# The MLP's first layer by one level of Strassen's method, with adding transfers, in four chunks

## The chip, the cores and the metric

One core of a Trainium2 chip runs the whole block for 512 tokens. The metric is the device time of one execution in microseconds (us): a median of 813.45 over 3 runs (813.43 to 813.47). Engines: TensorE (PE, with its weight loads PEld), VectorE (DVE), ScalarE (ACT), GpSimd (POOL), SyncE (SP, which only issues transfers).

## The reference

```python
h  = rmsnorm(x, norm_mix_g)
u, v, bg, cg, xs, ga, gb = split(h @ w_in)              # w_in: 1024 x 7168
a  = gelu(u) * (masked w_s @ rmsnorm(gelu(v)) + b_s)    # per 128-token block
c  = bg * causal_dwconv3(cg * xs)
m  = sigmoid(ga) * (a @ w_proj_a) + sigmoid(gb) * (c @ w_proj_b)
x  = x + m @ w_out
hf = rmsnorm(x, norm_ff_g)
z  = relu(hf @ w_ff1)                                   # w_ff1: 1024 x 4096
x  = x + (z * z) @ w_ff2                                # w_ff2: 4096 x 1024
return rmsnorm(x, norm_final_g)
```

All arrays are float32. x is 512 x 1024.

## The kernel before

Channels lie on the 128 partitions and the 512 tokens along the free axis, so a layer is a row of output tiles of 128 channels x 512 tokens, each summed over k tiles of 128 input channels. A float32 operand is carried as two float32r parts, hi (rounded) and lo (the rest), and a product is three matmuls: hi x hi, hi x lo of the activations, lo x hi (lines 120 to 122).

A weight *unit* is a 1024 x 128 block, one [128, 1024] tile: eight k tiles for one output tile, 24 matmuls. `prep` (line 97) loads it on SyncE's queue, ScalarE casts it to `whi` (line 84) and VectorE subtracts for `wlo` (line 85). `unit_matmuls` preps the unit it needs and two more ahead. Every engine takes its instructions in the order in which they stand on it.

The program goes through v, u with spatial gating, branch A's gate and projection, branch B, its gate and projection, the output projection (8 units), and the MLP. The MLP runs in `NCH` = 2 chunks of 16 hidden tiles. In a chunk the first layer makes 16 tiles: one unit each, then VectorE's ReLU times the token scale `Rf` out of PSUM (`t_z`, line 367), ScalarE's square (line 369) and the split into `zh` and `zl`. Then the second layer makes 8 output tiles from two units each and adds them to `res` (line 475). `x2h` and `x2l` (line 357) are the split input of the first layer. `Rf` comes from the sum of squares through `rstd_of` and `spread`, with a power on GpSimd (line 134). The last output tile is made in two halves of 256 tokens (`last_tile`, lines 424 to 426), so that the final norm of one half runs beside the other.

PSUM has seven banks in rotation and one for statistics. SBUF tiles are shared by phases through tags.

Of the kernel before, what the change touches and what calls it, by code (L numbers as in the profile page):

```python
# [8 lines left out]
F32 = mybir.dt.float32  # L9
# [12 lines left out]
NCH = 2  # L22
CF = FT // NCH
EPS = 1e-6
N_WARM = 10

# Columns of the packed per-channel vectors.
# [4 lines left out]
def hybrid_block(ctx, tc, xT, vecs, w_v, w_main, w_s, b_s, out_a, out_b):  # L32
# [12 lines left out]
    outp = ctx.enter_context(tc.tile_pool(name="outp", bufs=4))  # L45
# [4 lines left out]
    # ---------------------------------------------------------------- constants  # L50
# [14 lines left out]
    # TensorE reaches its full clock while the first loads are under way.  # L65
# [27 lines left out]
    # Every unit is [128 (k in tile), 8 (k tile), 128 (m)].  # L93
    n_units = w_main.shape[0]
    parts = {}

    def prep(i):
        if i >= n_units or i in parts:
            return
        r = raws.tile([P, KT * P], F32, name="raw")  # L100
        nc.sync.dma_start(r, w_main[i])
        hi = wsp.tile([P, KT * P], F32R, name="whi")
        lo = wsp.tile([P, KT * P], F32R, name="wlo")
        split_into(hi, lo, r)
        parts[i] = (hi, lo)

    state = {"next": 0}
    AHEAD = 2

    def unit_matmuls(psum, act_hi, act_lo, start=True, stop=True, cols=slice(0, S)):  # L110
        """psum += W_unit.T @ act over the unit's 8 k tiles."""
        i = state["next"]
        state["next"] += 1
        prep(i)
        for a in range(1, AHEAD + 1):
            prep(i + a)
        hi, lo = parts.pop(i)
        for k in range(KT):
            ks = slice(k * P, (k + 1) * P)
            nc.tensor.matmul(psum, hi[:, ks], act_hi[k][:, cols], start=start and k == 0, stop=False)  # L120
            nc.tensor.matmul(psum, hi[:, ks], act_lo[k][:, cols], start=False, stop=False)  # L121
            nc.tensor.matmul(psum, lo[:, ks], act_hi[k][:, cols], start=False, stop=stop and k == KT - 1)  # L122
# [14 lines left out]
    def rstd_of(acc, lo=0, n=NB):  # L137
        """Mean over partitions of acc's columns, as [token, block]; then rstd."""
# [7 lines left out]
    def spread(r, n=NB):  # L146
        """rstd as [token, block] -> [any partition, token], in PSUM."""
# [10 lines left out]
    xh = [shared("X", 16, f"xh{k}", F32R) for k in range(KT)]  # L158
    xl = [shared("X", 16, f"xl{k}", F32R) for k in range(KT)]
    acc = shared("acc", 1, "acc")  # L160
    vt = [[shared("V", 8, f"vt{b}{h}") for h in range(2)] for b in range(NB)]
    wsT = [shared("M", 16, f"wsT{i}").rearrange("p (g i) -> p g i", i=P) for i in range(2)]
    bsb = [shared("M", 16, f"bsb{i}").rearrange("p (g i) -> p g i", i=P) for i in range(2)]
    vsum = small.tile([P, 2, NB], F32, name="vsum")

    vparts = {}

    def prep_v(i):
        if i >= 2 * KT:
            prep(i - 2 * KT)  # L170
            return
# [3 lines left out]
        t = raws.tile([P, KT * P], F32, name="raw")[:, :HALF]  # L175
        nc.sync.dma_start(t, w_v[h, k])
        vh = shared("M", 16, f"vh{h}{k}", F32R)
        vl = shared("M", 16, f"vl{h}{k}", F32R)
# [30 lines left out]
    for i in range(2 * KT):  # L209
# [57 lines left out]
    def mix(g):  # L267
        pm = bank()
        for b in range(NB):
            nc.tensor.matmul(  # L270
                pm[:, b * P : (b + 1) * P], vt[b][g // 4][:, (g % 4) * P : (g % 4 + 1) * P], wsT[g // 4][:, g % 4, :],
# [5 lines left out]
            bsb[g // 4][:, g % 4 : g % 4 + 1, :].broadcast_to([P, NB, P]), op0=ALU.mult, op1=ALU.add,  # L277
# [43 lines left out]
    # ---------------------------------------------------------------- branch A's gate and projection  # L321
    m1 = [shared("V", 8, f"m1{k}") for k in range(KT)]
# [15 lines left out]
    mh = [shared("M", 16, f"mh{k}", F32R) for k in range(KT)]  # L338
    ml = [shared("M", 16, f"ml{k}", F32R) for k in range(KT)]
# [9 lines left out]
    # ---------------------------------------------------------------- output projection, residual  # L349
    xh2 = [shared("X", 16, f"x2h{k}", F32R) for k in range(KT)]  # L350
    xl2 = [shared("X", 16, f"x2l{k}", F32R) for k in range(KT)]
    acc = shared("acc", 1, "accb")
    for j in range(KT):
# [186 lines left out]
```

## Time and profile before

| | before |
|---|---|
| median of 3 runs | 813.45 us |
| span of the profiled execution | 811.9 us |
| granted TensorE clock, mean | 0.997 |
| first layer of the first chunk (456.0 to 545.4) | 89.4 us, TensorE busy throughout |
| second layer of the first chunk (545.4 to 632.4) | 87.0 us, TensorE busy throughout |
| mean DMA rate | 100 GB/s |

The span goes from the first to the last instruction; what lies around it (1.55 us against the median) has no rows. Busy times of PE are modelled from pipelined matmuls, so how far apart matmuls start says more than the duration of one.

### The profile page before, as it was taken

The page shows a single profiled execution, that of the slowest core. Times are in us where ns is not written, and L with a number is a line of the kernel's source. Part 1 is how long each engine was busy: PE and PEld are TensorE (multiplying, and loading weights), DVE is VectorE, ACT ScalarE, POOL GpSimd, SP SyncE. Part 2 cuts the span into 40 slices and gives each one's busy share as a digit, 9 for nine tenths or more (in the row PEclk, how much of TensorE's full clock was granted, in tenths as well). Part 3 has the DMA queues.
Part 4 walks back from the last instruction along what each step waited for, and adds up shares of the span by engine and source line. Part 5 has one row for each costly group of instructions (what it writes and reads, how often), then busy time and mean ns, then how long its engine had stood idle before and what let it go on. Part 6 is the DMA issues. An engine that isn't in the chain of part 4 may idle for free.

```text
span 811.9 us, 8874 instructions
## 1 busy us (share of the span) xinstructions
PE 804.2 (99%) x3646; PEld 667.2 (82%) x3646; DVE 376.0 (46%) x501; ACT 250.6 (31%) x324; POOL 6.1 (1%) x15
## 2 busy tenths in 40 slices
PE   9999999999999999999999999999999999999996
PEld 6888888888888888888888888888888888888886
DVE  7555653334555555444455554442233445434433
ACT  7323332222212222332344253332112334422221
POOL 0000000000000000000000000000000000000000
PEclk9999999999999999999999999999999999999998
DMA  7522223322332233233223223223322332233203
GB/s 247 195 105 104 78 77 105 104 90 92 104 104 82 100 105 103 79 104 103 93 89 105 97 84 105 101 81 104 103 93 89 105 103 85 97 104 104 79 0 105
DMA packets 25352, 81.35 MB, mean 100 GB/s; under 512 B 2768, under 2 KB 3792, under 8 KB 25312
## 3 DMA queue, kind: packets, MB, share of 16 engines
q1 hardware_dynamic: 24416, 79.18, 29.1%
q10 hardware_dynamic: 864, 1.57, 0.6%
q8 instruction: 28, 0.46, 0.3%
q14 instruction: 12, 0.10, 0.0%
q0 software_dynamic: 32, 0.03, 0.0%
HBM read 78.68 MB, written 2.10 MB: 99 GB/s over the span
## 4 chain that ended last, share of the span: by engine, by line
PE 98%; DMA 0%; ACT 0%; DVEq 0%; POOLq 0%; POOL 0%; DVE 0%; issue 0%
PE bank L121 30%; PE bank L120 30%; PE bank L122 30%; PE bank L219 5%; PE bank L270 1%; PE bank L425 0%; PE bank L426 0%; PE bank L424 0%; DMA res<-xT 0%; PE bank L152 0%; PE st L141 0%; DVEq L534 0%; PE bank L393 0%; PE st L441 0%; POOLq L534 0%; ACT xh L87 0%
## 5 line engine op out<-in xcount | busy, mean ns | idle before, releaser
L84 ACT CAST whi<-raw 128x1024 fp32r<-128x1024 f32 x136 | 143.4, 1054 | 494.2 <-PE bank L121 373.9
L85 DVE TENSOR_TENSOR wlo<-raw,whi 128x1024 fp32r<-128x1024 f32 x136 | 166.5, 1225 | 78.7 <-ACT whi L84 77.6
L120 PE MATMUL bank<-xh,whi 128*128 128x512 f32 x384 | 150.0, 391 | 0.0
L121 PE MATMUL bank<-xl,whi 128*128 128x512 f32 x384 | 149.4, 389 | 0.0
L122 PE MATMUL bank<-xh,wlo 128*128 128x512 f32 x384 | 149.4, 389 | 0.0
L120 PE MATMUL bank<-x2h,whi 128*128 128x512 f32 x256 | 99.8, 390 | 0.0
L122 PE MATMUL bank<-x2h,wlo 128*128 128x512 f32 x256 | 99.6, 389 | 0.0
L121 PE MATMUL bank<-x2l,whi 128*128 128x512 f32 x256 | 99.6, 389 | 0.0
L120 PE MATMUL bank<-zh,whi 128*128 128x512 f32 x240 | 93.4, 389 | 0.0
L121 PE MATMUL bank<-zl,whi 128*128 128x512 f32 x240 | 93.4, 389 | 0.0
L122 PE MATMUL bank<-zh,wlo 128*128 128x512 f32 x240 | 93.4, 389 | 0.0
L122 PEld LDWEIGHTS bank<-xh,wlo 128*128 128x128 f32 x384 | 72.1, 188 | 15.0
L120 PEld LDWEIGHTS bank<-xh,whi 128*128 128x128 f32 x384 | 72.2, 188 | 14.8
L121 PEld LDWEIGHTS bank<-xl,whi 128*128 128x128 f32 x384 | 72.1, 188 | 14.6
L367 DVE SCALAR_TENSOR_TENSOR t_z<-bank,Rf 128x512 f32<-128x512 f32 x32 | 22.0, 691 | 78.8 <-PE bank L122 78.8
L121 PEld LDWEIGHTS bank<-x2l,whi 128*128 128x128 f32 x256 | 48.1, 188 | 10.0
L122 PEld LDWEIGHTS bank<-x2h,wlo 128*128 128x128 f32 x256 | 48.1, 188 | 10.0
L120 PEld LDWEIGHTS bank<-x2h,whi 128*128 128x128 f32 x256 | 48.1, 188 | 9.9
L121 PEld LDWEIGHTS bank<-zl,whi 128*128 128x128 f32 x240 | 45.1, 188 | 9.4
L122 PEld LDWEIGHTS bank<-zh,wlo 128*128 128x128 f32 x240 | 45.1, 188 | 9.3
L120 PEld LDWEIGHTS bank<-zh,whi 128*128 128x128 f32 x240 | 45.1, 188 | 9.3
L475 DVE TENSOR_TENSOR res<-bank,res 128x512 f32<-128x512 f32 x15 | 10.4, 692 | 50.1 <-PE bank L122 50.1
(118 smaller groups left out, 818.6 us busy)
## 6 DMA issues: line engine op xcount, KB each, us to landing
raw<-w_main SPq DMA_DIRECT2D x136, 512.0 KB, 3.2
raw<-w_v SPq DMA_DIRECT2D x16, 256.0 KB, 4.0
res<-xT SPq DMA_DIRECT2D x8, 256.5 KB, 4.8
out_a<-o SPq DMA_DIRECT2D x4, 256.0 KB, 2.4
wsT<-w_sT ACTq DMA_DIRECT2D x2, 256.0 KB, 5.0
bsb<-b_sb ACTq DMA_DIRECT2D x2, 256.0 KB, 5.5
out_b<-ob ACTq DMA_DIRECT2D x2, 256.0 KB, 3.0
out_b<-ob SPq DMA_DIRECT2D x2, 256.0 KB, 3.1
```

The lines of the kernel that those rows point to most:

```text
L84: nc.scalar.copy(hi, src)
L85: nc.vector.tensor_tensor(lo, src, hi.bitcast(F32), op=ALU.subtract)
L120: nc.tensor.matmul(psum, hi[:, ks], act_hi[k][:, cols], start=start and k == 0, stop=False)
L121: nc.tensor.matmul(psum, hi[:, ks], act_lo[k][:, cols], start=False, stop=False)
L122: nc.tensor.matmul(psum, lo[:, ks], act_hi[k][:, cols], start=False, stop=stop and k == KT - 1)
L219: nc.tensor.matmul(vbanks[h][b], xs[k][:, b * P : (b + 1) * P], ws, start=k == 0 and ws is vh and xs is xh, stop=k == KT - 1 and xs is xl,)
L270: nc.tensor.matmul(pm[:, b * P : (b + 1) * P], vt[b][g // 4][:, (g % 4) * P : (g % 4 + 1) * P], wsT[g // 4][:, g % 4, :], start=True, stop ...
L367: nc.vector.scalar_tensor_tensor(t, pz, 0.0, Rf, op0=ALU.max, op1=ALU.mult)
L475: nc.vector.tensor_add(res[j], py, res[j])
```

## The change

The first layer's product W1^T x is cut into 2 x 2 blocks and made with 7 block products in place of 8, in the form with shared sums. Two output tiles of 128 channels, from a 1024 x 256 block of W1, are a *pair*; its four blocks are 512 x 128 (four slices of 128 input channels each, stored as `w_ff1[i]` = A12, A11, A22, A21, where the first index is the output tile and the second the half of the input channels). The right sides are the halves of the input channels x halves of the tokens, so every matmul has 256 columns.

- `combos` makes the right sides once, in the output projection, whose units come in the order 0, 4, 1, 5, ... so that both halves are at hand: B11, B21 and B22 as they are, and four sums (nT1, T3, nT2, nT4). Each is split in hi and lo.
- A pair has four *operands* of weights: raw A12 and A11; raw A22; and two tiles of sums. The two sums in `sm[0]` (a `wsum` tile) are made by transfers on GpSimd's queue: `build` copies A11 and A22 into it and then adds A21 to both with an adding transfer. The other two, in `sm[1]`, are made by VectorE (`add2`, lines 470 and 471). `wsum0` and `wsum2` take turns as targets of the transfers, `wsum1` and `wsum3` as VectorE's.
- `add_operand`, `pump` and `need` make the splits a list of steps, of which each product or unit takes one. At most `RING` = 4 operands are held.
- `block_pair` runs the seven products (`product`, 4 slices x 3 matmuls). The last one, P7, and what follows it, run after the next pair's P2 (`late`). Results leave PSUM through copies on ScalarE and sums on VectorE into `c1` and `c2`, and `z_evac` goes on from there in SBUF.
- The MLP has four chunks of 8 hidden tiles (4 pairs) and 8 second-layer units. Each chunk but the last also makes the first pair of the next. The last two output tiles, not one, are made in halves.
- A load on SyncE's queue now brings two units (1 MB), or three blocks of a pair (768 KB). `raws` has two such buffers.

```diff
-NCH = 2
+NCH = 4
+RING = 4
...
-    raws = ctx.enter_context(tc.tile_pool(name="raws", bufs=4))
-    wsp = ctx.enter_context(tc.tile_pool(name="wsp", bufs=3))
+    raws = ctx.enter_context(tc.tile_pool(name="raws", bufs=2))
+    wsp = ctx.enter_context(tc.tile_pool(name="wsp", bufs=RING))
...
+    def add_operand(src, n=2, last=None):
+        o = {"done": False, "ready": False, "idx": len(opnds)}
+        def step():
+            hi = wsp.tile([P, n, S], F32R, name="whi", padded_shape=[P, 2, S])
+            lo = wsp.tile([P, n, S], F32R, name="wlo", padded_shape=[P, 2, S])
+            split_into(hi, lo, src())
+            o["hi"], o["lo"], o["ready"] = hi, lo, True
+            if last:
+                load_after(last)
+        opnds.append(o)
+        steps.append((step, o))
+        return o
+
+    def pump(n=1):
+        while steps and n:
+            step, o = steps[0]
+            if o is not None and o["idx"] >= RING and not opnds[o["idx"] - RING]["done"]:
+                return
+            steps.pop(0)
+            step()
+            n -= 1
...
+    def build(i):
+        if i < NP1:
+            t = sums_t[2 * (i % 2)]
+            nc.gpsimd.dma_start(t, w_ff1[i, :, 1:3, :])
+            nc.gpsimd.dma_start(t, w_ff1[i, :, 3:4, :].broadcast_to([P, 2, S]), accum_op=ALU.add)
...
+            def add2(raw=raw, sm=sm, key=key):
+                nc.vector.tensor_tensor(sm[1][:, 1, :], sm[0][:, 1, :], raw(1, 2)[:, 0, :], op=ALU.add)
+                nc.vector.tensor_tensor(sm[1][:, 0, :], sm[1][:, 1, :], raw(0, 1)[:, 0, :], op=ALU.add)
+                load_after(key)
+            tl = []
+            tl.append(add_operand(lambda raw=raw: raw(0, 2)))
+            tl.append(add_operand(lambda raw=raw: raw(2, 3), n=1))
+            steps.append((add2, None))
+            tl.append(add_operand(lambda sm=sm: sm[1]))
+            tl.append(add_operand(lambda sm=sm: sm[0]))
+            steps.append((lambda i=i: build(i + 2), None))
+            pairs.append(tl)
+
+    LEFT = {"P1": (0, 1, "B11"), "P2": (0, 0, "B21"), "D": (1, 0, "nT4"), "F": (2, 0, "B22"),
+            "P6": (2, 1, "nT2"), "E": (3, 1, "nT1"), "P7": (3, 0, "T3")}
+
+    def product(p, name, out, first, last=False):
+        t, g, r = LEFT[name]
+        o = pairs[p][t]
+        pump()
+        need(o)
+        for sl in range(KS):
+            c = slice(sl * P, (sl + 1) * P)
+            w_hi, w_lo = o["hi"][:, g, c], o["lo"][:, g, c]
+            x_hi, x_lo = right[r, sl, 0], right[r, sl, 1]
+            nc.tensor.matmul(out, w_hi, x_hi, start=first and sl == 0, stop=False, skip_group_check=True)
+            nc.tensor.matmul(out, w_hi, x_lo, start=False, stop=False, skip_group_check=True)
+            nc.tensor.matmul(out, w_lo, x_hi, start=False, stop=sl == KS - 1, skip_group_check=True)
+        if name in ("P2", "D", "P6", "P7"):
+            o["done"] = True
...
+    def block_pair(p, after):
+        ba, bf, bd = bank(), bank(), bank()
+        A, P2 = ba[:, :N2], ba[:, N2:]
+        F = bf[:, :N2]
+        Dp, E = bd[:, :N2], bd[:, N2:]
+        c1, c2 = temp("c1"), temp("c2")
+        product(p, "P1", A, True)
+        product(p, "P2", P2, False)
+        nc.scalar.copy(c1[:, :N2], A)
+        nc.vector.tensor_add(c1[:, :N2], P2, c1[:, :N2])
+        flush_late()
+        product(p, "D", Dp, True)
+        product(p, "F", F, True)
+        product(p, "P6", A, False)
+        nc.scalar.copy(c1[:, N2:], A)
+        nc.vector.tensor_add(c1[:, N2:], F, c1[:, N2:])
+        product(p, "E", E, False)
+        def end():
+            product(p, "P7", A, False)
+            nc.vector.tensor_add(c1[:, N2:], E, c1[:, N2:])
+            nc.scalar.copy(c2[:, :N2], A)
+            nc.vector.scalar_tensor_tensor(c2[:, N2:], E, -1.0, c2[:, :N2], op0=ALU.mult, op1=ALU.subtract)
+            nc.vector.tensor_sub(c2[:, :N2], Dp, c2[:, :N2])
+            after(c1, c2)
+        late.append(end)
...
-    for j in range(KT):
+    for n in range(KT):
+        j = n // 2 + 4 * (n % 2)
         po = bank()
         unit_matmuls(po, mh, ml)
         nc.vector.tensor_add(res[j], po, res[j])
-        split_into(xh2[j], xl2[j], res[j], scale=col(V_GFF, j))
-        sum_squares(acc, res[j], j)
+        xg[j] = temp("xg")
+        nc.scalar.activation(xg[j], res[j], AF.Copy, scale=col(V_GFF, j))
+        if n % 2:
+            combos(j - 4, xg.pop(j - 4), xg.pop(j))
+        sum_squares(acc, res[j], n)
...
     for ck in range(NCH):
-        zh = [shared("AC", 16, f"zh{ck}_{i}", F32R) for i in range(CF)]
-        zl = [shared("M", 16, f"zl{ck}_{i}", F32R) for i in range(CF)]
...
+        end = min((ck + 1) * CF // 2 + 1, NP1)
+        for p in range(done, end):
+            ff1_pair(p)
+        done = end
+        flush_late()
+        zh, zl = zip(*[z_tile(ck * CF + i) for i in range(CF)])
```

The next rows are VectorE's in the first layer before, for three tiles: a split of a weight unit, a split of z, and the ReLU out of PSUM.

```order
L85 TENSOR_TENSOR wlo_4708<-raw_4705,whi_4707 128x1024
L85 TENSOR_TENSOR zl1_6_4435<-q_4700,zh1_6_4419 128x512
L367 SCALAR_TENSOR_TENSOR t_z_4735<-bank_4704,Rf_3272 128x512
L85 TENSOR_TENSOR wlo_4745<-raw_4742,whi_4744 128x1024
L85 TENSOR_TENSOR zl1_7_4436<-q_4737,zh1_7_4420 128x512
L367 SCALAR_TENSOR_TENSOR t_z_4772<-bank_4741,Rf_3272 128x512
```

And now, twelve of a pair's fifteen, between pairs 2 and 3. `c1_3456` and `c2_3457` belong to pair 2, `c1_3583` to pair 3; `raw_3460` is pair 4's, `wsum2` holds pair 3's transferred sums, `wsum1` is pair 4's VectorE sum.

```order
L580 SCALAR_TENSOR_TENSOR c1_3456<-c1_3456,Rf_3196 128x512
L471 TENSOR_TENSOR wsum1_2848<-wsum1_2848,raw_3460 128x512
L96 TENSOR_TENSOR wlo_3644<-wsum2_2849,whi_3643 128x1024
L519 TENSOR_TENSOR c1_3583<-bank_3580,c1_3583 128x256
L532 SCALAR_TENSOR_TENSOR c2_3457<-bank_3455,c2_3457 128x256
L96 TENSOR_TENSOR zm2_3201<-c1_3456,zm2_3201 128x512
L533 TENSOR_TENSOR c2_3457<-bank_3455,c2_3457 128x256
L96 TENSOR_TENSOR wlo_3674<-raw_3460,whi_3673 128x1024
L580 SCALAR_TENSOR_TENSOR c2_3457<-c2_3457,Rf_3196 128x512
L96 TENSOR_TENSOR wlo_3692<-raw_3460,whi_3691 128x512
L96 TENSOR_TENSOR wlo_3729<-wsum1_2848,whi_3728 128x1024
L525 TENSOR_TENSOR c1_3583<-bank_3581,c1_3583 128x256
```

Ahead of these stands L470 of pair 4, which reads the transferred `wsum0`; behind them come a split of z, L530 of pair 3, and L580. Splits of weights stand between the emptyings of PSUM, one pair ahead of their use.

GpSimd's queue held five small powers and one load of vectors. Before, the three powers ahead of the final norm stood together:

```order
L134 TENSOR_TENSOR r4_354<-ms4_352,expo_96 128x4
L134 TENSOR_TENSOR r4_565<-ms4_563,expo_96 128x4
L134 TENSOR_TENSOR r4_3343<-ms4_3341,expo_96 128x4
L134 TENSOR_TENSOR r2_5587<-ms2_5585,expo_96 128x2
L134 TENSOR_TENSOR r2_5661<-ms2_5659,expo_96 128x2
```

Now copies (L452) and adding transfers (L453) of the pairs stand between them; from pair 2 on each pair's two follow each other.

```order
L203 TENSOR_TENSOR r4_523<-ms4_521,expo_93 128x4
L452 DMA wsum0_2847<-w_ff1 128x1024
L452 DMA wsum2_2849<-w_ff1 128x1024
L453 DMA wsum0_2847<-w_ff1 128x2x512
L453 DMA wsum2_2849<-w_ff1 128x2x512
L452 DMA wsum0_2847<-w_ff1 128x1024
L453 DMA wsum0_2847<-w_ff1 128x2x512
L203 TENSOR_TENSOR r4_3317<-ms4_3315,expo_93 128x4
L452 DMA wsum2_2849<-w_ff1 128x1024
L453 DMA wsum2_2849<-w_ff1 128x2x512
```

The power for `Rf` (`r4_3317`) has moved behind pair 2's two transfers.

## Rows read from the trace of the kernel before

**Rows 1.** The page, busy time: engine, us, share of the span, instructions.

```profile
PE 804.2 (99%) x3646; PEld 667.2 (82%) x3646; DVE 376.0 (46%) x501; ACT 250.6 (31%) x324; POOL 6.1 (1%) x15
```

**Rows 2.** The page, chain of work that ended last, by engine.

```profile
PE 98%; DMA 0%; ACT 0%; DVEq 0%; POOLq 0%; POOL 0%; DVE 0%; issue 0%
```

**Rows 3.** Busy time by stretch: the first chunk's first layer, then its second.

```profile
core 0: us, PE busy (x) PEld busy (x) DVE busy (x) ACT busy (x) POOL busy (x), PEclk, DMA share, GB/s
456.00:545.40 89.40, 89.40 (x404) 74.29 (x403) 42.54 (x54) 36.05 (x49) 1.01 (x1) 1.00 0.28 95
545.40:632.40 87.00, 87.00 (x385) 72.06 (x385) 25.54 (x25) 16.84 (x17) 0.00 (x0) 1.00 0.29 97
```

**Rows 4.** TensorE in order of time (start, duration), where columns go from 512 to 256.

```profile
788.88 0.39 PE L120 MATMUL bank<-zh,whi 128*128 128x512 f32 x1
789.11 0.39 PE L121 MATMUL bank<-zl,whi 128*128 128x512 f32 x1
789.34 0.39 PE L122 MATMUL bank<-zh,wlo 128*128 128x512 f32 x1
789.56 0.28 PE L424 MATMUL bank<-zh,whi 128*128 128x256 f32 x1
789.68 0.28 PE L425 MATMUL bank<-zl,whi 128*128 128x256 f32 x1
...
796.28 0.28 PE L426 MATMUL bank<-zh,wlo 128*128 128x256 f32 x1
```

**Rows 5.** VectorE's groups by line and shape: count | busy us, mean ns | idle before.

```profile
L85 DVE TENSOR_TENSOR wlo<-raw,whi 128x1024 fp32r<-128x1024 f32 x136 | 166.5, 1225 | 78.7 <-ACT whi L84 77.6
L85 DVE TENSOR_TENSOR zl<-q,zh 128x512 fp32r<-128x512 f32 x32 | 22.2, 693 | 1.4 <-ACT zh L84 1.4
L367 DVE SCALAR_TENSOR_TENSOR t_z<-bank,Rf 128x512 f32<-128x512 f32 x32 | 22.0, 691 | 78.8 <-PE bank L122 78.8
L192 DVE TENSOR_TENSOR accf<-accf,sq 128x256 f32<-128x256 f32 x12 | 4.5, 419 | 0.5 <-ACT sq L191 0.5
L429 DVE TENSOR_TENSOR res<-bank,res 128x256 f32<-128x256 f32 x2 | 0.8, 425 | 4.3 <-PE bank L426 4.3
```

**Rows 6.** VectorE in order of time: a dependent pair, then two independent instructions.

```profile
267.90 1.54 DVE L297 SCALAR_TENSOR_TENSOR y<-z,vec,y 128x512 f32<-128x512 f32 x2
269.48 0.69 DVE L301 TENSOR_TENSOR yr<-y,R 128x512 f32<-128x512 f32 x1
...
458.77 1.22 DVE L85 TENSOR_TENSOR wlo<-raw,whi 128x1024 fp32r<-128x1024 f32 x1
459.91 0.28 DVE L151 TENSOR_SCALAR dg<-ident,r 128x128 f32<-128x128 f32 x1
```

**Rows 7.** ScalarE's groups by line and shape.

```profile
L84 ACT CAST whi<-raw 128x1024 fp32r<-128x1024 f32 x136 | 143.4, 1054 | 494.2 <-PE bank L121 373.9 <-issue 113.1 <-DMA raw<-w_main 7.3
L369 ACT ACTIVATE q<-t_z 128x512 f32<-128x512 f32 x32 | 20.0, 626 | 2.7 <-DVE t_z L367 2.6
L84 ACT CAST zh<-q 128x512 fp32r<-128x512 f32 x32 | 19.9, 622 | 1.0
L191 ACT ACTIVATE sq<-res 128x256 f32<-128x256 f32 x12 | 4.3, 408 | 5.3 <-DVE res L475 5.3
```

**Rows 8.** Transfers: line or tile, queue, count, KB each, median us from issue to landing.

```profile
raw<-w_main SPq DMA_DIRECT2D x136, 512.0 KB, 3.2
out_a<-o SPq DMA_DIRECT2D x4, 256.0 KB, 2.4
vec<-vecs POOLq DMA_DIRECT2D x1, 32.0 KB, 3.4
```

**Rows 9.** GpSimd's one issue of a transfer, as a group by line and shape.

```profile
L52 POOL DMA_DIRECT2D vec<-vecs x1 | 0.7, 708 | 0.8 <-POOLq L529 0.8
```

**Rows 10.** SyncE's issues of weight loads: duration ns, least, median, most; starts.

```profile
L101 SPq DMA_DIRECT2D raw<-w_main x136: 327/328/328, 27.2 to 764.7; - x136
```

**Rows 11.** The span and the mean granted clock.

```profile
core 0: 811.9 us, clock 0.997
```

More of the change, by code (lines that the diff above doesn't have):

```diff
@@ L94, in hybrid_block @@
     n_units = w_main.shape[0]
-    parts = {}
-    def prep(i):
-        if i >= n_units or i in parts:
-            return
[L100 to L105, printed above, removed]
-    state = {"next": 0}
[L108 to L122, printed above, removed]
+    steps = []
@@ new lines, in hybrid_block, with load, load_after @@
+    opnds = []
+    raw_of = {}
+    def load(key):
+        if key in raw_of:
+            return
+        r = raws.tile([P, 4, S], F32, name="raw")
+        kind, i = key
+        if kind == "u":
+            nc.sync.dma_start(
+                r.rearrange("p (u a) s -> p u (a s)", u=2), w_main[i : i + 2].rearrange("u p f -> p u f")
+            )
+        else:
+            nc.sync.dma_start(r[:, :3, :], w_ff1[i, :, :3, :])
+        raw_of[key] = r
+    loads = []
+    def load_after(key):
+        n = loads.index(key) + 2
+        if n < len(loads):
+            load(loads[n])
@@ new lines, in pump, with need, plan_units @@
+    def pump(n=1):
[6 more added lines that the diff above has]
+            n -= 1
+    def need(o):
+        while not o["ready"]:
+            steps.pop(0)[0]()
+    units = []
+    def plan_units(n):
+        for _ in range(n // 2):
+            i = len(units)
+            key = ("u", i)
+            loads.append(key)
+            for e in range(2):
+                units.append(add_operand(
+                    lambda key=key, e=e: raw_of[key][:, 2 * e : 2 * e + 2, :], last=key if e else None
+                ))
@@ new lines, in hybrid_block, with unit_matmuls @@
+    state = {"next": 0}
+    def unit_matmuls(psum, act_hi, act_lo, start=True, stop=True, cols=slice(0, S), ks=range(KT), o=None):
+        if o is None:
+            o = units[state["next"]]
+            state["next"] += 1
+            pump()
+            need(o)
+            o["done"] = True
+        hi, lo = (o[h].rearrange("p a s -> p (a s)") for h in ("hi", "lo"))
+        for k in ks:
+            c = slice(k * P, (k + 1) * P)
+            first, end = start and k == 0, stop and k == KT - 1
+            nc.tensor.matmul(psum, hi[:, c], act_hi[k][:, cols], start=first, stop=False)
+            nc.tensor.matmul(psum, hi[:, c], act_lo[k][:, cols], start=False, stop=False)
+            nc.tensor.matmul(psum, lo[:, c], act_hi[k][:, cols], start=False, stop=end)
@@ L174, in prep_v @@
             nc.sync.dma_start(resg[k], xT[k])
-        t = raws.tile([P, KT * P], F32, name="raw")[:, :HALF]
+        if i % 2 == 0:
+            vraw.append(wide("AC", f"vraw{i}"))
+        t = vraw[-1][:, i % 2, :]
         nc.sync.dma_start(t, w_v[h, k])
-        vh = shared("M", 16, f"vh{h}{k}", F32R)
-        vl = shared("M", 16, f"vl{h}{k}", F32R)
+        if i == 2 * KT - 1:
+            for key in loads[:2]:
+                load(key)
+        vp = wide("M", f"vp{h}{k}", F32R)
+        vh, vl = vp[:, 0, :], vp[:, 1, :]
         if h == 0:
@@ L319, in hybrid_block @@
             mix(j - LAG)
[L322 removed]
+    m1p = halves_of("V", "m1", F32, KT // 2)
+    m1 = [m1p[k % 2][k // 2] for k in range(KT)]
     for j in range(KT):
@@ L352, in hybrid_block @@
+    plan_pairs(CF // 2 + 1)
+    for ck in range(NCH):
+        plan_units(KT)
+        if ck < NCH - 1:
+            plan_pairs(CF // 2 - (ck == NCH - 2))
     acc = shared("acc", 1, "accb")
-    for j in range(KT):
+    xg = {}
+    for n in range(KT):
+        j = n // 2 + 4 * (n % 2)
         po = bank()
@@ L407, in finish_second, with last_tiles @@
                 eng.dma_start(out_b[n, :, h * HALF : (h + 1) * HALF], o)
-    def last_tile(j):
-        i0 = state["next"]
-        state["next"] += 2
-        prep(i0)
-        prep(i0 + 1)
+    def last_tiles(js):
+        us = units[state["next"] : state["next"] + len(js)]
+        state["next"] += len(js)
+        for o in us:
+            need(o)
         todo = []
```

199 lines of the change are left out of this document (124 added, 75 removed).

## Prediction

> **What bounds the kernel now.** I read the busy time first: TensorE is busy for 804.2 of 811.9 us, VectorE for 376.0, ScalarE for 250.6 [rows 1]. A busy share alone does not prove a bound, so the chain of waits comes second: followed back from the end, 98% of it is TensorE [rows 2]. Third, the stretches of the MLP: in the first layer TensorE has no idle microsecond, VectorE works 42.5 of 89.4 us, ScalarE 36.1, and the DMA engines are taken to 0.28; in the second layer VectorE drops to 25.5 of 87.0 [rows 3]. So here time is only won by giving TensorE less to do, and lost when another engine makes it wait. The clock was granted in full (1.00, the 2.4 GHz level) through both [rows 3].
>
> **TensorE's part.** The first layer was 32 tiles x 24 = 768 matmuls of 512 columns. They start 0.2267 us apart (789.56 - 788.88 is three of them) [rows 4]: 768 x 0.2267 = 174.1 us. Now each of 16 pairs of tiles takes 7 products x 4 slices x 3 = 84 matmuls of 256 columns, 1344 in all. Such matmuls exist already, in the last tile: 56 steps from 789.56 to 796.28 are 0.120 us each [rows 4], with a weight load beside every one, as there will be. 1344 x 0.120 = 161.3 us, so a pair takes 10.08 us, a product 1.44, and **12.8 us go**. One eighth of the work would be 21.8; the rest is the fixed part of a matmul, which now comes twice. The second layer keeps its 768 tile matmuls (48 of them cut in two, as before), in four chunks instead of two, and these add no matmul.
>
> The Trainium skill (TensorE: Matmul & The Clock Gate, Back-to-back issue gap) gives N / 2.4 + 2.5 ns, or 216 and 109 ns, which would make the saving 18.9 us. The rows say 227 and 120 for these operands, and they decide.
>
> **VectorE and ScalarE per pair.** I count VectorE's 15 instructions of a steady pair from the order: three splits of 128x1024 at 1.225 us, seven operations on 512 columns at 0.69 (one split, two block sums, two of ReLU times Rf, two splits of z), five on 256 columns at 0.42 [rows 5]. That is 3.68 + 4.83 + 2.10 = 10.6 us, more than TensorE's 10.08. But an instruction that does not need the one before starts about 0.08 us before that one's end (a split of 1.22 us is followed after 1.14), while one that needs it starts 0.04 after [rows 6]. I take 15 x 0.08 off: 9.4 us. VectorE then fits, with 0.7 us to spare. Before, the same work for two tiles was 2 x 2.61 = 5.2 us. ScalarE: three casts at 1.054, one at 0.622, three copies of 256 columns at about 0.41, and 2 x (0.626 + 0.622) for z [rows 7]: 7.5 us, hidden. In the output projection the new combinations bring VectorE to 2 x 1.225 + 7 x 0.69 + 5 x 0.42 = 9.4 of 10.9 us for two units, also hidden. Behind the last unit eleven VectorE instructions stand up to the last combination (cmv3, four of 256 columns, five of 512, two splits), 6.9 us with the overlaps, where TensorE asks for it after 45 matmuls = 5.4: 1.5 us of wait. At the last chunk no pair lies between z and its use: I take 0.4 us.
>
> **The adding transfers.** This is the new wait. For each pair GpSimd issues a copy of two blocks (512 KB) into a sum tile, waits until it has landed, and issues the transfer that adds a third block to both (512 KB read, and 512 KB of the sums read back). Call the time from release to landing W. It is released when VectorE has split the sum of the pair two before (fourth operand of pair i), and wanted by L470 for pair i+2. In the order between those two stand eleven VectorE instructions, and behind L470 on the same queue stand L580, L471 and the next fourth operand, which releases the next transfers. So one turn of the loop is W + 0.61 + 0.61 + 0.61 + 1.23 = W + 3.1 us, and it must not exceed TensorE's 10.08: **W up to 7.0 us is free**. Behind the waiting L470 stands all else that VectorE does for TensorE: the next splits, and the emptying of PSUM.
>
> Nothing in the trace shows an adding transfer, nor a large one from GpSimd's queue. From below: 512 KB on SyncE's queue land in 3.2 us, and an add as quick as a copy makes W = 6.4. For a value: a GpSimd issue takes 0.71 us against 0.33 on SyncE, so a copy is 3.6; 256 KB land in 2.4 and 512 in 3.2, so 0.8 us per further 256 KB, and the add moves 512 KB more: 3.6 + 1.6 = 5.2. **W = 8.8** [rows 8 to 10]. From above: if the add takes each 256 KB as slowly as a transfer by itself, 4 x 2.4 = 9.6, and W = 13.2. I take 8.8, the value whose parts are all rows of quiet queues. Bandwidth as such is no limit: a pair moves 1.8 MB where two tiles moved 1.05, so 0.28 becomes about 0.5.
>
> The Trainium skill (Collectives: The Full Stack, section on bandwidth, "Why ReduceScatter is half of AllGather") holds that an add in the transfer costs a second source read and not the addition. That is the way I sized the middle value; no row here shows it.
>
> What W costs, chunk by chunk, with TensorE's time counted from the end of the unit before:
> - First chunk (pairs 0 to 4; transfers 2, 3, 4 in the loop). The fourth operand of pair 0 is split at 2.3 us, and transfer 2 lands at W + 2.3. From L470 to the next fourth operand it is 5.5 us this once (the split for F and Rf lie between), then twice W + 3.1, then 2.9 us to the first operand of pair 4: 3W + 17.0. TensorE is there at 8.64 + 3 x 10.08 = 38.9. Wait 3W - 21.9 = 4.5 us; the 1.5 us above is within it.
> - Second and third chunk (two transfers in the loop each). The fourth operand of the first pair is ready at 2.4, and its slot lets the next one be ready at 15.3 at the soonest (W + 5.9 if that is later, from W = 9.4). Then W + 3.1, and 2.9 to the first operand of the last pair: W + 21.3 against 8.64 + 2 x 10.08 = 28.8. Wait W - 7.5 = 1.3 us each, above W = 9.4 it is 2W - 16.9.
> - Last chunk (one transfer): W + 8.7 against 18.7, so nothing up to W = 10.
>
> Other transfers of the first layer are issued while the second runs, where they have 40 us.
>
> **The sum.** -12.8 + 4.5 + 1.3 + 1.3 + 0.4 = -5.3 us. The profiled execution spans 811.9 us [rows 11], and 1.55 us lie around that against the median of 813.45, which I leave as they are: 806.6 + 1.55 = **808.2 us**. Start, branches, output projection and end keep their matmuls; the 1 MB weight loads have the same four units of buffer, and come every 10.9 us.
>
> **Rivals.**
> - *The transfers are hidden.* W is 7 or less, TensorE alone sets the pair. For it: the two 3.2 us landings [rows 8]. Against it: a second wait on the way through GpSimd, slower to issue, and the extra read. Left are 1.5 + 0.4 us of wait: 813.45 - 12.8 + 1.9 = 802.6. A formula of the Trainium skill (DMA: Bandwidth & Descriptors, Anatomy of one DMA), 2.0 us + bytes / 436 GB/s, puts W at 3.2 + 4.4 = 7.6 as an estimate, nearly there; its 3.2 for 512 KB agrees with the row.
> - *The transfers set the pace, and the kernel gets slower.* One mechanism: VectorE stands at L470 while the add lands. It decides from where the waits eat the gain: (3W - 21.9) + 2 x (2W - 16.9) + 0.4 = 12.8, W = 9.7. At W = 11.5 the waits are 12.6 + 2 x 6.1 + 1.5 + 0.4 = 26.7, and the time 827.4. For it: the add is unmeasured, it comes in 2 KB pieces, the weight load of the next pair (768 KB) is issued only 1.2 us before the copy, and 0.9 us over my W is enough. Against it: each part of the 8.8 comes from a row.
> - *VectorE binds.* If the starts do not overlap, a pair takes 10.6 us: 16 x 0.5 = 8.6 us with the 1.9 above, 811.2. For it: several of the fifteen wait for ScalarE or for their predecessor. Against it: the second layer gives VectorE 3.5 us of rest per unit, and each chunk starts four operands ahead.
> - *The halves run slower than 0.120.* In the rows the weight loads never show as a gap over 56 steps; at 0.130 the saving would be gone. I give it next to nothing.
>
> **Chances.** Forecast (W from 7 to 9.7) 0.36, hidden 0.26, transfers set the pace 0.28, VectorE binds 0.10. Within 0.2% (1.6 us) is no difference that can be measured. Hidden is faster throughout, and so is most of the forecast's case (up to W = 9.4) and half of VectorE's: 0.62 faster; around W = 9.7 and in VectorE's case the same, 0.09; slower 0.29. The forecast's own range is 803 to 812. For 8 in 10 I go from just under the hidden case, 801, to W = 11.2: 825.
>
> **What would show it.** First layer's stretches: matmuls of 256 columns 0.120 us apart, pairs 10.1 us long where nothing waits. VectorE's waits: L470 waiting for a transfer, eight times at most, a few microseconds each; none would mean the hidden case. The landing of the two transfers, which gives W directly. If TensorE waits where L470 does not, VectorE binds. I am wrong if the matmuls' spacing is not 0.120, if waits appear in the second layer or the branches, or if W is outside 6.4 to 13.2.

## The result and the profile after

The changed kernel takes **833.1 us** (median of 4 runs, 832.15 to 833.58) against 813.46 before (4 runs on the same chip): a ratio of **1.0237**, 95% interval 1.0225 to 1.025. It is slower; forecast was 808.2, and 833.1 lies outside the range. The profiled execution spans 831.8 us at a mean granted clock of 0.988 [rows 11].

The page's busy times and its chain by engine, after:

```profile
PE 801.6 (96%) x4222; PEld 691.9 (83%) x4222; DVE 465.2 (56%) x686; ACT 294.3 (35%) x420; POOL 34.8 (4%) x47
...
PE 83%; DMA 8%; DVE 4%; issue 4%; ACT 0%; POOL 0%; POOLq 0%; DVEq 0%
```

TensorE's share went from 99 to 96% [rows 1], and the chain, once 98% TensorE [rows 2], runs for 8% through transfers and for 4% through VectorE. The waits of the changed kernel say where (us in total, times, longest):

```profile
DVE wsum L470 <- DMA wsum<-w_ff: 36.4, 8, 6.1
PE bank L497 <- DVE c L519: 22.2, 7, 4.3
PE bank L498 <- DVE cmv L96: 0.4, 1, 0.4
```

One turn of that loop in the first chunk, GpSimd, then VectorE, then TensorE in order of time (start, us):

```profile
482.15 0.59 POOL L452 DMA_DIRECT2D wsum<-w_ff  x1 [8.55 <-DVE wlo L96]
487.14 1.19 POOL L453 DMA_DIRECT2D wsum<-w_ff  x1 [4.39 <-DMA wsum<-w_ff]
...
487.78 0.42 DVE L530 TENSOR_TENSOR c<-bank,c 128x256 f32<-128x256 f32 x1
493.33 0.69 DVE L470 TENSOR_TENSOR wsum<-wsum,raw 128x512 f32<-128x512 f32 x1 [5.14 <-DMA wsum<-w_ff]
493.94 0.68 DVE L580 SCALAR_TENSOR_TENSOR c<-c,Rf 128x512 f32<-128x512 f32 x1
494.54 0.68 DVE L471 TENSOR_TENSOR wsum<-wsum,raw 128x512 f32<-128x512 f32 x1
495.14 1.22 DVE L96 TENSOR_TENSOR wlo<-wsum,whi 128x1024 fp32r<-128x1024 f32 x1
496.28 0.42 DVE L519 TENSOR_TENSOR c<-bank,c 128x256 f32<-128x256 f32 x1
...
496.75 0.39 PE L497 MATMUL bank<-cmb,whi 128*128 128x256 f32 x1 [4.17 <-DVE c L519]
496.97 0.28 PE L498 MATMUL bank<-cmb,whi 128*128 128x256 f32 x1
...
498.08 0.41 PE L497 MATMUL bank<-cmv,whi 128*128 128x256 f32 x1
498.30 0.42 PE L498 MATMUL bank<-cmv,whi 128*128 128x256 f32 x1
```

The copy is issued when its target is free (482.15) and the add when the copy has landed (487.14). L470 starts when the add has landed: **W** = 493.33 - 482.15 = 11.18 us. Behind L470 stand three more instructions and then L519, which frees the PSUM that TensorE's product P6 wants: TensorE stands for 4.17 us. The last two lines show something else: behind the wait matmuls start about 0.21 us apart, not 0.12. Stretches of TensorE behind waits (columns as in [rows 3]):

```profile
482.00:486.00 4.00, 3.76 (x31) 3.76 (x32) 4.00 (x8) 2.86 (x5) 0.59 (x1) 1.00 0.41 133
498.00:501.00 3.00, 3.00 (x16) 3.00 (x15) 3.00 (x4) 2.25 (x4) 0.12 (x1) 0.50 0.53 169
590.00:592.00 2.00, 2.00 (x11) 2.00 (x11) 2.00 (x4) 0.98 (x2) 0.00 (x0) 0.50 0.73 248
```

The granted clock is 0.50, the 1.2 GHz level, behind the waits that end at 496.75 and 588.98, and 1.00 behind the one of 3.40 us that ends at 482.24. In the whole MLP I count 88 *slow steps*, by which I mean 0.17 to 0.25 us from the start of one matmul of 256 columns to the next; over 0.120 each they add 8.2 us.

The landings (issue to landing) of the copies (L452), then of the adds (L453), least, median and most, where SyncE's 512 KB took 3.2 before [rows 8]:

```profile
DMA to landing us min/median/max: 3.6/4.0/4.7
```

```profile
DMA to landing us min/median/max: 5.3/7.8/9.8
```

One correction to [rows 3]: by the operands of its matmuls, the first chunk's first layer before runs from 450.4 to 539.3 and its second from there to 626.4; the stretches given start about 6 us late. VectorE's share hardly changes by it (43.2 of 88.9 us).

### The profile page after: what moved, and what is told of

The parts are those of the page before. It is cut to its first block, busy times and chain, and to the rows that moved or that the text cites. A ratio compares the mean times of both kernels' runs of the same rounds, so it can differ in the third digit from the quotient of the medians.

```text
span 831.8 us, 10213 instructions
## 1 busy us (share of the span) xinstructions
PE 801.6 (96%) x4222; PEld 691.9 (83%) x4222; DVE 465.2 (56%) x686; ACT 294.3 (35%) x420; POOL 34.8 (4%) x47
## 4 chain that ended last, share of the span: by engine, by line
PE 83%; DMA 8%; DVE 4%; issue 4%; ACT 0%; POOL 0%; POOLq 0%; DVEq 0%
PE bank L189 23%; PE bank L190 23%; PE bank L191 23%; DMA wsum<-w_ff 8%; PE bank L302 5%; PE bank L497 3%; PE bank L498 3%; PE bank L499 3%; DVE wlo L96 2%; PE bank L351 1%; PE st L75 1%; ACT whi L95 0%; DVE c L580 0%; DVE wsum L471 0%; POOL wsum L452 0%
## 5 line engine op out<-in xcount | busy, mean ns | idle before, releaser
L95 ACT CAST whi<-raw 128x1024 fp32r<-128x1024 f32 (+1 forms) x136 | 135.0, 1002 | 347.4 <-PE bank L190 305.1
L96 DVE TENSOR_TENSOR wlo<-raw,whi 128x1024 fp32r<-128x1024 f32 (+1 forms) x136 | 157.6, 1159 | 18.3 <-ACT whi L95 17.8
L189 PE MATMUL bank<-x,whi 128*128 128x512 f32 x384 | 150.0, 391 | 0.0
L190 PE MATMUL bank<-x,whi 128*128 128x512 f32 x384 | 149.5, 389 | 0.0
L191 PE MATMUL bank<-x,wlo 128*128 128x512 f32 x384 | 149.5, 389 | 0.0
L497 PE MATMUL bank<-cmb,whi 128*128 128x256 f32 x256 | 75.7, 296 | 22.2 <-DVE c L519 22.2
L190 PEld LDWEIGHTS bank<-x,whi 128*128 128x128 f32 x384 | 72.1, 188 | 14.9
L189 PEld LDWEIGHTS bank<-x,whi 128*128 128x128 f32 x384 | 72.1, 188 | 14.6
L189 PE MATMUL bank<-zm,whi 128*128 128x512 f32 (+1 forms) x204 | 77.1, 378 | 0.0
L191 PE MATMUL bank<-zm,wlo 128*128 128x512 f32 (+1 forms) x204 | 76.9, 377 | 0.0
L190 PE MATMUL bank<-zm,whi 128*128 128x512 f32 (+1 forms) x204 | 76.9, 377 | 0.0
L499 PE MATMUL bank<-cmb,wlo 128*128 128x256 f32 x256 | 74.3, 290 | 0.0
L498 PE MATMUL bank<-cmb,whi 128*128 128x256 f32 x256 | 74.3, 290 | 0.0
L497 PEld LDWEIGHTS bank<-cmb,whi 128*128 128x128 f32 x256 | 51.0, 199 | 24.9 <-DVE c L519 23.6
L498 PEld LDWEIGHTS bank<-cmb,whi 128*128 128x128 f32 x256 | 51.3, 200 | 0.0
```

Source lines behind the costliest of these rows:

```text
L189: nc.tensor.matmul(psum, hi[:, c], act_hi[k][:, cols], start=first, stop=False)
L190: nc.tensor.matmul(psum, hi[:, c], act_lo[k][:, cols], start=False, stop=False)
L191: nc.tensor.matmul(psum, lo[:, c], act_hi[k][:, cols], start=False, stop=end)
L497: nc.tensor.matmul(out, w_hi, x_hi, start=first and sl == 0, stop=False, skip_group_check=True)
L498: nc.tensor.matmul(out, w_hi, x_lo, start=False, stop=False, skip_group_check=True)
L499: nc.tensor.matmul(out, w_lo, x_hi, start=False, stop=sl == KS - 1, skip_group_check=True)
```

## Experiments

Theory A: with two targets, VectorE stands at L470 for the transfers and TensorE behind it. Theory B: VectorE's own work binds. Further experiments ask why the add takes 7.8 us, and what the clock costs. All edits are against the changed kernel where nothing else is said, and `...` stands for lines left out.

**e1: three targets for the transfers, one tile for VectorE's sums.**

```diff
-            t = sums_t[2 * (i % 2)]
+            t = sums_t[i % 3]
...
     build(1)
+    build(2)
...
-            sm = [sums_t[2 * (i % 2) + e] for e in range(2)]
+            sm = [sums_t[i % 3], sums_t[3]]
...
-            steps.append((lambda i=i: build(i + 2), None))
+            steps.append((lambda i=i: build(i + 3), None))
```

> Three tiles take turns as targets of the transfers and VectorE's two sums use the fourth, so a pair's transfers are released a whole pair earlier; the same instructions otherwise. Theory A (VectorE stands at L470 for the transfers, W = 12 to 13 us): W is free up to about 2 x 10.08 - 3.1 = 17 us, so the waits at L470 vanish, TensorE's clock stays at its upper level in the MLP, and the time falls from 833 to 802 to 805 us. Theory B (VectorE has too much to do per pair, and the waits at L470 only show where it lies idle anyway): pairs stay longer than 10.08 us; with 10.6 us per pair the time is 811, and with 14 as now it stays near 833. Theory C (halves of 256 columns are slower than 0.120 us): time stays near 833 with no waits.

Measured 802.93 us, ratio 0.9868 (0.9852 to 0.9885), clock 0.997. The adds land no sooner (median 7.9, up to 12.6 us), yet no instruction waits for them. TensorE's one wait in the first layer, 0.4 us, is near its start. Busy times, and VectorE's first operation of two turns:

```profile
PE 792.5 (99%) x4222; PEld 683.8 (85%) x4222; DVE 466.0 (58%) x686; ACT 292.9 (37%) x420; POOL 34.8 (4%) x47
```

```profile
476.00 1.23 DVE L96 TENSOR_TENSOR wlo<-wsum,whi 128x1024 fp32r<-128x1024 f32 x1
486.08 1.23 DVE L96 TENSOR_TENSOR wlo<-wsum,whi 128x1024 fp32r<-128x1024 f32 x1
```

A pair takes 10.08 us. Theory A is shown: the same transfers, released one pair further ahead, cost nothing.

**e3: all four sums on VectorE, no transfers of GpSimd.**

```diff
-            nc.sync.dma_start(r[:, :3, :], w_ff1[i, :, :3, :])
+            nc.sync.dma_start(r, w_ff1[i])
...
-            nc.gpsimd.dma_start(t, w_ff1[i, :, 1:3, :])
-            nc.gpsimd.dma_start(t, w_ff1[i, :, 3:4, :].broadcast_to([P, 2, S]), accum_op=ALU.add)
...
+                nc.vector.tensor_tensor(sm[0][:, 0, :], raw(1, 2)[:, 0, :], raw(3, 4)[:, 0, :], op=ALU.add)
+                nc.vector.tensor_tensor(sm[0][:, 1, :], raw(2, 3)[:, 0, :], raw(3, 4)[:, 0, :], op=ALU.add)
```

> No transfers on GpSimd's queue: the fourth block is loaded with the other three and VectorE makes all four sums, two more operations on 512 columns per pair. Theory A: VectorE then has 9.4 + 1.2 = 10.6 us per pair against TensorE's 10.08, so it binds lightly: 16 x 0.5 + 1.9 us of waits, 810 to 813 us, far under 833. Theory B: VectorE was already what binds, so this is slower than 833.

Measured 802.73 us, ratio 0.9867 (0.9852 to 0.9882): a miss of the expectation. VectorE is all but full, and TensorE waits 0.4 us (columns as in [rows 3]):

```profile
450.00:502.00 52.00, 51.62 (x428) 51.14 (x426) 50.20 (x83) 33.53 (x55) 1.32 (x1) 1.00 0.24 82
```

Two more operations per pair than in the change, and still TensorE does not wait for VectorE from pair to pair: what a pair lacks is taken from the lead that VectorE has when the chunk begins. The trace shows that lead shrink: the split of a pair's third operand ends 5.4, 4.2, 2.7 and 1.4 us ahead of its use in pairs 1 to 4, where in e1 it is 5.1 and then steadily 4.8. Theory B falls.

**e4: the kernel before with four chunks** (the edit is against the kernel before).

```diff
-NCH = 2
+NCH = 4
...
-                unit_matmuls(py, zh[0:8], zl[0:8], stop=False)
-                unit_matmuls(py, zh[8:16], zl[8:16], start=False)
+                unit_matmuls(py, zh, zl)
```

> The kernel before with the MLP in four chunks and nothing else changed (one unit instead of two per output tile and chunk). The count of matmuls is the same and VectorE adds 24 more times into res, beside idle time: 813.5 us, within 1. If chunk borders cost TensorE something (z of a chunk's last tiles not ready), up to 2 us per new border, 817.

Measured 815.28, ratio 1.0022 (1.0012 to 1.0031): this edit costs 1.0 to 2.5 us. Its trace has two waits of TensorE more than before, 1.3 us in the statistics at the end and 0.7 at the start of the program, which account for all of that; there is none at a border of chunks. e1 waits 0.4 at the start and not in the statistics at the end, so this cost says little about the changed kernel.

**e2: the second transfer a plain copy** (so these sums are left out of the computation).

```diff
-            nc.gpsimd.dma_start(t, w_ff1[i, :, 3:4, :].broadcast_to([P, 2, S]), accum_op=ALU.add)
+            nc.gpsimd.dma_start(t, w_ff1[i, :, 3:4, :].broadcast_to([P, 2, S]))
```

> The second transfer of each pair copies its 512 KB in place of adding them, in the same pieces and behind the same wait; the sums are left out. Theory A with the add as the long part (7.8 us to land, of which a copy of the same bytes would take 4 to 4.5): W = 8.5 to 9, waits 3W - 21.9 in the first chunk and W - 7.5 in the next two, 6 to 8 us in all, and no loss of clock: 806 to 809 us. If the pieces or GpSimd's queue make it long and not the add, the transfer lands in 7 to 8 us as before and the time stays near 833. Theory B: little change, over 820.

Measured 820.22, ratio 1.0077 (1.0062 to 1.0092): between the two. The landings of the second transfer:

```profile
DMA to landing us min/median/max: 4.1/5.7/7.7
```

The median is 5.7 us instead of 7.8. So the addition accounts for about 2 us of the landing (1.6 of W on the mean), but a plain copy in its place takes 1.7 us more than the first copy's 4.0.

**e5: the added block stored twice, read in 4 KB pieces, not 2 KB.**

```diff
-            nc.gpsimd.dma_start(t, w_ff1[i, :, 3:4, :].broadcast_to([P, 2, S]), accum_op=ALU.add)
+            nc.gpsimd.dma_start(t, w_ff1[i, :, 3:5, :], accum_op=ALU.add)
...
-        g = np.stack([a[1, 2], a[1, 1], a[2, 2], a[2, 1]], 2)
+        g = np.stack([a[1, 2], a[1, 1], a[2, 2], a[2, 1], a[2, 1]], 2)
```

> The block that is added is stored twice, so that the adding transfer reads 4 KB pieces in place of 2 KB ones; nothing else changes. The adding transfers of the changed kernel landed in 5.3 to 9.8 us (median 7.8), a copy in the same 2 KB pieces in 4.1 to 7.7 (median 5.7), a copy in 4 KB pieces in 4.0. Theory of the pieces: the add falls by about 1.7 us to some 6.1, the turn of VectorE's loop from W = 11.5 to 9.8, the waits by about ten us: 818 to 824. Theory of the loads beside (SyncE's weight loads share the DMA engines with the add) and theory of the add itself: the landing stays within 0.5 us of 7.8, the time within 829 to 834.

Measured 834.11, ratio 1.0256 (1.0236 to 1.0276); the adds land in 5.2 to 10.0 us, median 7.8. The pieces are not what makes the add long.

**e8: the MLP's own loads on SyncE's queue left out** (two earlier weight tiles are used again).

```diff
+        kind, i = key
+        if kind == "p" or i >= n_plain:
+            raw_of[key] = raw_of[loads[loads.index(key) - 2]]
+            return
         r = raws.tile([P, 4, S], F32, name="raw")
-        kind, i = key
```

> The MLP's own loads on SyncE's queue (raw weights of the pairs and of the second layer) are left out, and the last two weight tiles loaded before it are used again in their place; the two transfers per pair on GpSimd's queue stay. Theory of the loads beside: every adding transfer lands in about 5.3 us, as the one of the changed kernel did that had the queue to itself (456.9 to 462.2), W is about 9.2 in every pair, the waits are 3 x 9.2 - 21.9 = 5.7 in the first chunk, 1.7 in the second and third each and none in the last, 9 us in all, and the time 811 to 817. Theory of the add itself: landings keep a median of 7.8 and the time stays at 829 to 834.

The landings of all its adds:

```profile
DMA to landing us min/median/max: 5.3/5.4/9.0
```

The median falls from 7.8 to 5.4, and 14 of the 16 land in 5.3 to 5.7: the loads beside make the rest. In the changed kernel such a load of 1 MB is issued at 485.82, just ahead of the add of 487.14, and the DMA engines are full from 488 to 492 while the two run (columns as in [rows 3], DMA share last but one):

```profile
485.82 0.38 SPq L118 DMA_DIRECT2D raw<-w_main  x1
```

```profile
486.00:488.00 2.00, 2.00 (x19) 2.00 (x19) 2.00 (x4) 0.63 (x2) 0.86 (x1) 1.00 0.63 102
488.00:490.00 2.00, 2.00 (x19) 2.00 (x18) 0.19 (x1) 1.32 (x2) 0.33 (x1) 1.00 0.98 403
490.00:492.00 2.00, 2.00 (x19) 2.00 (x18) 0.00 (x0) 0.00 (x0) 0.00 (x0) 1.00 1.12 216
```

The time, 825.95 (ratio 1.0159, 1.0128 to 1.019), is far over the 811 to 817 expected, for two reasons. In its first chunk, where VectorE's order is that of the change, W is 8.9, 9.9 and 10.4 and not 9.2, since the copies take 4.6 and 5.0 us from release to the add's issue even here; and from then on VectorE's order differs and it waits for 14 adds in place of 8. Its time is no measure of the loads alone.

**e10: two plain copies in 4 KB pieces** (e2 and e5 together; the sums are left out).

```diff
-            nc.gpsimd.dma_start(t, w_ff1[i, :, 3:4, :].broadcast_to([P, 2, S]), accum_op=ALU.add)
+            nc.gpsimd.dma_start(t, w_ff1[i, :, 3:5, :])
...
-        g = np.stack([a[1, 2], a[1, 1], a[2, 2], a[2, 1]], 2)
+        g = np.stack([a[1, 2], a[1, 1], a[2, 2], a[2, 1], a[2, 1]], 2)
```

> Both transfers of a pair are plain copies in 4 KB pieces (the block that was added is stored twice, and the sums are left out); the order on every engine is that of the changed kernel. The second copy in 2 KB pieces landed in 5.7 us (median) and the time was 820.2. If the pieces made that 5.7, the second copy now lands in some 4.3 like the first, W is 4.4 + 4.3 = 8.7 or so, under the turn at which the waits eat the gain (9.7), and the time lies under that of the kernel before: 806 to 812. If the loads beside it made it (as the add's own landing did not change with the pieces), it stays at 5.7 and the time at 819 to 822.

Measured 815.83, ratio 1.0023 (1.0014 to 1.0033); the second copy lands in 3.7 to 6.2 us, median 5.3. Neither theory: the longer pieces take 0.4 us off the landing and not 1.4, W falls from e2's 9.7 only to 9.3 on the mean, and even so the time is over that before.

**e6: the changed kernel with matmuls in the places of its waits.**

```diff
+    FILL = {2: 28, 3: 36, 6: 18, 7: 40, 10: 22, 11: 38, 14: 22}
...
+        o = pairs[p][2]
+        for k in range(FILL.get(p, 0)):
+            sl = k % KS
+            nc.tensor.matmul(bf[:, N2:], o["hi"][:, 0, sl * P : (sl + 1) * P], right["B22", sl, 0],
+                             start=False, stop=False, skip_group_check=True)
         product(p, "P6", A, False)
```

> The changed kernel with extra matmuls of 256 columns in front of P6 in the seven pairs where TensorE waited (28, 36, 18, 40, 22, 38 and 22 of them, 204 x 0.120 = 24.5 us), written to the unused half of F's bank; they change no result. They stand where TensorE waited 22.2 us. If the granted clock fell because TensorE had stood idle, it stays at 0.997 here, and matmuls stay 0.120 us apart behind the former waits. What that brings tells whether the clock was a loss by itself: if so, the time falls by up to 7.5 us, to 826 to 829. If the transfers set the pace of the pairs anyway, a slow TensorE was only a shorter wait at the next pair, and the time stays at 831 to 835. If the clock falls all the same, the waits are not its cause.

Measured 846.17, ratio 1.0398 (1.0383 to 1.0414): inconclusive on the time. The extra matmuls also changed the order in which VectorE's instructions stand in the first layer, and waits of 5.34 and 3.91 us came back in other places. Of the 49 slow steps now, 35 stand right behind those two; in the other five filled places no more than two slow steps follow each other.

**e7: e3 with pauses of TensorE; e9: e3 with matmuls in their places** (the edits are against e3; e7's first).

```diff
+    PAUSE = {1: 4, 2: 5, 3: 6, 6: 7, 7: 8, 10: 9, 11: 10, 14: 12}
...
+        for k in range(PAUSE.get(p, 0)):
+            nc.gpsimd.tensor_tensor(gap, gap if k else c1[:, :NB], zero if k == 0 else half, op=ALU.mult if k == 0 else ALU.pow)
+        if p in PAUSE:
+            nc.tensor.matmul(A[:, 0:1], ones, gap[:, 0:1], start=False, stop=False, skip_group_check=True)
         product(p, "P6", A, False)
```

```diff
+    FILL = {1: 4, 2: 13, 3: 21, 6: 29, 7: 38, 10: 46, 11: 54, 14: 71}
...
+        o = pairs[p][2]
+        for k in range(FILL.get(p, 0)):
+            c = slice(k % KS * P, (k % KS + 1) * P)
+            nc.tensor.matmul(bf[:, N2:], o["hi"][:, 0, c], right["B22", k % KS, 0],
+                             start=False, stop=False, skip_group_check=True)
```

> The version in which VectorE makes all four sums (802.73 us, no waits of TensorE in the first layer), with a pause of TensorE put in front of P6 in eight pairs: one matmul of one column, which adds zero, waits for a chain of 4, 5, 6, 7, 8, 9, 10 and 12 small operations of about 1.0 us on GpSimd, whose queue is otherwise empty here. The chain starts when VectorE has written c1, some 3.5 us ahead of P6, so the pauses are about 0.5, 1.5, 2.5, 3.5, 4.5, 5.5, 6.5 and 8.5 us, 33 in all. If a pause costs only itself, the time is 802.7 plus the pauses that the trace shows, 836. If TensorE's granted clock falls behind a longer pause, as it did in the changed kernel, then matmuls stand 0.21 us apart for a few microseconds behind it, and about 1 us comes on top of each, 840 to 845. The ladder shows the shortest pause of this kernel behind which the clock fell.

> The same version (VectorE makes all sums), with extra matmuls of 256 columns (4, 13, 21, 29, 38, 46, 54 and 71, 276 x 0.120 = 33.1 us) in the eight places where the other run has pauses; they write to the unused half of F's bank and change no result. Clock theory: granted clock 0.997, spacing 0.120 throughout, time 802.7 + 33.1 = 835.8 and less than the run with pauses by what the clock costs there. If the clock falls for another reason than waiting, it falls here too and both runs have the same time.

e9 takes 836.29 (ratio 1.0276, 1.0261 to 1.0292): 802.73 and the 33.1 us of its matmuls give 835.8, and the clock is 0.997. e7 takes 874.24 (1.0738, 1.072 to 1.0756). Its pauses came out longer than meant, in total and count:

```profile
PE bank L533 <- POOL gap L531: 52.7, 8, 11.6
```

Two of its pauses, 0.97 and 4.12 us, and the clock in the stretches behind them:

```profile
469.90 0.38 PE L533 MATMUL bank<-gap,ones 128*128 128x1 f32 x2 [0.97 <-POOL gap L531]
484.58 0.58 PE L533 MATMUL bank<-gap,ones 128*128 128x1 f32 x2 [4.12 <-POOL gap L531]
```

```profile
470.00:474.00 4.00, 4.00 (x34) 4.00 (x35) 2.63 (x5) 2.23 (x4) 0.00 (x0) 1.00 0.68 256
485.00:490.00 5.00, 5.00 (x24) 5.00 (x25) 1.47 (x3) 2.00 (x4) 0.00 (x0) 0.50 0.01 3
```

802.73 + 52.7 = 855.4; 18.8 us come on top of the pauses themselves. Of these 13.9 are in the 149 slow steps of its trace, where e3 has 14 that cost 1.4; some 3.4 are the one-column matmuls themselves, and the rest is not resolved. Behind each of the seven pauses of 4.12 us and more the clock fell, behind 0.97 us it did not. Kept busy in the same places for 0.5 to 8.5 us (e9), TensorE kept its clock. A wait of TensorE of some microseconds costs more than its length.

## Why the prediction was wrong

**The failed step is the size of the adding transfers: "W = 8.8", as 3.6 for the copy and 5.2 for the add.** For the eight waits of L470, W is 11.3 on the mean: 4.4 from release to the add's issue, 6.9 from there to L470. The 5.2 itself is right where the queue is quiet. The first add of the first chunk, which a load joins only at 460.05, lets L470 start 5.3 us after its issue, and so do most of e8's:

```profile
456.85 1.19 POOL L453 DMA_DIRECT2D wsum<-w_ff  x1 [3.27 <-DMA wsum<-w_ff]
460.05 0.33 SPq L122 DMA_DIRECT2D raw<-w_ff  x1
462.15 0.69 DVE L470 TENSOR_TENSOR wsum<-wsum,raw 128x512 f32<-128x512 f32 x1 [1.54 <-DMA wsum<-w_ff]
```

That size was in part luck, since its 0.8 us per 256 KB sets stores of 256 KB (`out_a`) against loads of 512 KB [rows 8]. I took "the value whose parts are all rows of quiet queues" while I had counted that a weight load is issued next to each copy. That load was named as a reason for the slow rival and given no price. In the trace a load runs beside every one of the eight adds, four times 768 KB for a pair and four times 1 MB for the second layer, which the prediction did not set beside an add. What the loads cost the add: 5.4 against 7.8 at the median (e8). "Bandwidth as such is no limit" looked at a mean: the DMA share of the changed kernel's first chunk is 0.51, as forecast, but 0.98 and 1.12 in the two stretches above where a load and an add run together. The copy's further 0.8 us is there without the loads too (e8's first chunk). A part of it goes with the stored weights: with four blocks per pair, copies of odd pairs land in about 4.0 us into any target and with or without loads (13 of 16 in e1 and e8), and those of even pairs mostly in 3.2 to 3.6; with five blocks (e10) most of both land in about 3.7. Why is open.

The Trainium skill (Collectives: The Full Stack, section on the bandwidth ceiling, "Why ReduceScatter is half of AllGather") says of ReduceScatter that its add costs a second source read and not the addition. The quiet add agrees with the size that I drew from that, 5.3 against 5.2, but no run here separates the read from the addition.

**The law for the waits was right in the sum.** I put the W of each of the eight waits into the forecast's terms: in the first chunk the sum of three W less 21.9, in the second and the third the sum of two less 16.9, in the last its W less 10, none below nothing. Against them stand TensorE's waits in the first layer, with what the slow steps add:

| kernel | mean W | waits by the terms | waits measured | slow steps | time |
|---|---|---|---|---|---|
| e1, three targets | | | 0.4 | 0.8 | 802.9 |
| e10, two copies | 9.3 | 9.1 | 9.1 | 5.0 | 815.8 |
| e2, copy for add | 9.7 | 11.6 | 11.4 | 6.6 | 820.2 |
| e5, long pieces | 11.2 | 24.1 | 22.1 | 8.2 | 834.1 |
| changed kernel | 11.3 | 24.6 | 22.6 | 8.2 | 833.1 |

All us. 802.9 - 0.4 - 0.8 = 801.7 is the time without either; with the waits and slow steps of each row it makes 815.8, 819.7, 832.0 and 832.5. So nearly all of the 30 us between the changed kernel and e1 are named. Taken by chunk the law is rougher: the first chunk comes out 1 to 3 us too long in all four, the others are within 1.3.

**The second step missed is the clock.** I priced a wait at its length and said nothing of what comes behind it. The slow steps cost 8.2 us here, 7.4 over those of e1. So the 24.9 us between 808.2 and 833.1 fall in two: waits of 24.6 + 0.4 by the prediction's own terms in place of 7.5 make 17.5, and 825.7 us, and the clock makes the other 7.4. (That this meets 833.1 to the tenth is luck: the terms are 2.0 us over the waits measured.) The slow steps also move the point from which the change loses: by the terms it is W = 9.7, and with 9.3 e10 is already 2 us slower than before. The rival's time for W = 11.5, 827.4, is short by about this.

**The rest, point by point.** TensorE's saving: spacing of 0.120 us [rows 4] and 10.08 us per pair, as forecast; the fourth rival did not come. The chain and the place of the loss are those of the second rival (the transfers set the pace): L470, eight waits. VectorE: 9.4 us per pair by starts [rows 5, 6] was forecast; in e1 it stands 0.59 us in a turn of 10.08, which leaves 9.49. The third rival (VectorE binds) fell, and e3 shows that the lead at a chunk's start, which I had named, is worth more than I gave it. The hidden case, 802.6, is e1's 802.93, though not by my parts: the start of the first layer waits 0.4 us and not 1.5, the 0.4 of the last chunk did not come, and the slow steps that e1 has too (0.8) were not in the sum; some 1 us is not named. Two sums of the prediction are slightly off and change nothing: the saving put at 18.9 us is 19.0 by its own formula, and 16 x 0.5 is 8.0 (8.5 with 10.61 for a pair), not 8.6.

## What to carry to other kernels

Where a transfer stands in a loop with the engine that waits for it, size it with the transfers that run beside it, and count how many turns ahead it is started: one more target took away every wait for them without making the transfer shorter. Before paying a slower path to spare an engine, try the engine: VectorE had room for the sums, if only thanks to its lead. And a wait of TensorE of some microseconds mostly costs its length and a slow stretch behind it.

## What the runs showed of the hardware

- TensorE's granted clock fell to 0.50, its 1.2 GHz level, behind idle times: matmuls of 256 columns then start 0.213 us apart instead of 0.120, for 2.5 to 5.8 us. In the changed kernel it fell behind idle times of 2.27, 2.44, 3.70, 4.17 and 4.35 us and not behind 1.85 and 3.40; in e7 behind all from 4.12 to 11.57 and not behind 0.97. Why the one of 3.40 was spared is open; waits of 3.49 in e2 and e5 were not.
- An adding transfer of 512 KB on GpSimd's queue lands in 5.3 to 5.7 us alone (14 of e8's 16) and mostly in 6.2 to 8.9 beside loads of 768 KB or 1 MB (13 of the changed kernel's 16).
- The pieces set what an issue takes GpSimd: an adding transfer 1.19 us in 2 KB pieces and 0.86 in 4 KB pieces (e5), a plain copy 0.71 (e2) and 0.53 to 0.62. They hardly set the landing (e5, e10).
